# Finer steps of a state-space precomputation in the first MLP, and q times old states for four heads in a row

## The chip, the cores and the metric

The kernel runs on one core of a Trainium2 chip. A core has TensorE (matmuls; PE in the profile, its weight loads PEld), VectorE (DVE), ScalarE (ACT), GpSimd (POOL) and SyncE (SP, which issues most DMAs here). The metric is the device time of one execution in microseconds, the median of the runs.

## The reference

One step of a two-layer decoder: 256 prompt tokens of one sequence and 8 sequences with 4 new tokens each, so 288 columns in all, with 2048 features.

```python
def trunk(x, c, pos, s_gla, s_ret, s5_re, s5_im, ...):
    sc = jax.nn.silu(c)
    for l in range(2):
        mod = jnp.einsum('bd,sde->sbe', sc, w_ada[l]) + b_ada[l][:, None, :]   # shift, scale, gate
        h = modulate(rmsnorm(x, norm_pre[l, 0]), sh0, scl0)
        if l == 0:   # 4 GLA heads and 4 RetNet heads, dk 128, dv 256
            y, ng, nr = gla_retnet_mixer(h, pos, s_gla, s_ret, ...)
        else:        # diagonal complex state space: 128 groups x 64 states
            y, nre, nim = s5_mixer(h, s5_re, s5_im, lam_re, lam_im, log_dt, b, c, d, w_glu_a, w_glu_b)
        x = x + gt0[:, None, :] * rmsnorm(y, norm_post[l, 0])
        h = modulate(rmsnorm(x, norm_pre[l, 1]), sh1, scl1)
        m = jnp.square(jax.nn.relu(h @ w_mlp_up[l])) @ w_mlp_down[l]           # 2048 -> 8192 -> 2048
        x = x + gt1[:, None, :] * rmsnorm(m, norm_post[l, 1])
```

In the mixer of layer 0 each head has a state S (128 x 256) for each sequence. The 4 new tokens of a sequence give `o = att @ v + q_in @ S` and `S = decay * S + k_out^T v`. In layer 1 the discretised coefficients (exp, sin and cos of lambda times dt, their powers and their products with b and c) depend on weights alone; they are computed in the kernel all the same.

## The kernel before

Activations are kept with features on partitions: tiles of 128 x 2 x 288. A weight product is made from three fp32r matmuls (lines 242 to 244: high part by high part, low activation by high weight, high activation by low weight). For that each weight load of 1 MB (512 x 512) is split by ScalarE into `wh` (line 220) and by VectorE, sometimes GpSimd, into `wl` (line 222). **A weight slot** is one such load: 48 matmuls of 128 x 128 by 288 columns, 16 of each line.

The stages in order: condition vectors (`ada_stream`, matmuls of line 254), input projection, attention and output projection of layer 0 (64 slots), the first MLP, the state-space layer, the second MLP.

In these stages the order of TensorE's and SP's instructions is the order of the program text (`manual_schedule`); that of VectorE, ScalarE and GpSimd comes from a planner, which takes what is ready by its own estimates. Each engine then works off its queue in order. Nearly all temporary tiles of 128 x 576 come from one pool, `c2`, of 53 buffers; a new tile waits until the one that had its buffer is done with.

*The first MLP* (`Mlp.run`) has, after a head of 4 slots, 124 slots, here numbered from 0: groups u = 1 to 15 of four "up" slots (n = 0 to 3) and four "down" slots (n = 0 to 3), and four last down slots. After the up slots of a group `hidden` makes relu, its square, and its parts hi and lo (lines 579, 580, 228, 230). In the down slots products are added to accumulators (lines 649 for the first group, 651 after). At fixed places of a slot one step is taken of a generator, `drain(side, 1)`: a step runs up to the next `yield`.

*The side generator* is `s5_pre`, in this order: four steps of small VectorE instructions (128 x 64) that depend on each other; 32 steps (4 groups, 4 powers m, real and imaginary) in each of which GpSimd makes a product `fb` and an array `fz` (lines 1436 to 1442), with TensorE's transposes of `fz` (line 1378), ScalarE's copy `ft`, four DMAs from SP's queue and, for every second, TensorE's lag matmuls (line 1396) with a DMA from GpSimd's queue (line 1406), one or two steps later; then 8 steps of `lc` (lines 1464 to 1467: for each of four powers four products, a sum and a DMA on GpSimd); and 8 steps of tables `tc`, `ts` (lines 1475 to 1490: six doublings of six operations each on GpSimd, two copies and two DMAs).

*Old states* (`samples`, once for GLA and once for RetNet): for each of 4 groups `gb` of two sequences and each of 4 heads, TensorE multiplies q by the old state (line 953, two matmuls of fp32, each recorded as two passes, into the 32 columns of the array that belong to the head) and makes k^T v in PSUM (line 957); VectorE decays the state and adds it (line 961 or 965), GpSimd issues the store (line 966). The masks `km` of a group are two VectorE operations (line 923). The generator `attention` that contains it is advanced by `fill_in`, four times a slot; a step that yields 1.3 uses up 1.3 calls. Steps that are left when the output projection needs the result (ahead of slots 48 and 56 of the 64, numbered from 0) are all taken at once.

Of the kernel before, what the change touches and what calls it, by code (L numbers as in the profile page):

```python
# [13 lines left out]
OP = mybir.AluOpType  # L14
# [9 lines left out]
DK, DV, H = 128, 256, 4  # L24
# [132 lines left out]
def build(tc, nc, d):  # L157
# [27 lines left out]
    def bank(shape=(128, 512)):  # L185
        return bp.tile(list(shape), F32, name=nm("b"), tag="b")
# [311 lines left out]
    class Mlp:  # L498
# [53 lines left out]
        def run(self, r, fill, last=False, side=None, after=None, prep=(None, None)):  # L552
            l = self.l
            sub = Sub(l, 1)
            hid, acc, hv = {}, {}, {}
            slots = []
            for u in range(1, 17):
                slots += [("up", u, n) for n in range(4) if u < 16] + [("dn", u - 1, n) for n in range(4)]
            due = [0.0]

            def fill_in(rate):
                due[0] += rate
                while due[0] > 0:
                    due[0] -= next(fill, None) or 1

            def w_load(i):
                if i < len(slots):
                    k, u, n = slots[i]
                    self.raw[i] = load(d["g_up"][l, u, n] if k == "up" else d["g_dn"][l, n, u])

            def w_split(i):
                if i < len(slots):
                    hv[i] = split_w(self.raw.pop(i))

            def hidden(u, ps):
                hid[u] = []
                for pr in range(2):
                    t = c2("relu")
                    A.activation(t, ps[pr][:, :, :NT], AF.Relu)  # L579
                    V.tensor_mul(t, t, t)  # L580
                    hid[u].append(split_a(t))

            acts, ps = self.head(r, fill)
            with tc.manual_schedule(engines={E_.PE, E_.SP}):
                w_load(0)
                w_load(1)
                w_split(0)
                hidden(0, ps)
                for i, (k, u, n) in enumerate(slots):
                    w_load(i + 2)  # L590
                    w_split(i + 1)
                    if k == "up":
                        for pr in range(2):
                            if n == 0:
                                ps[pr] = pair()
                            gran_mm(ps[pr], hv[i], pr, acts[4 * n:4 * n + 4], n == 0, n == 3)
                            fill_in(0.28 if side else 0.3)
                        if n == 3:
                            hidden(u, ps)
                        if side and n:  # L600
                            drain(side, 1)
                    else:
                        if n == 0:
                            ops = chunks(hid.pop(u))
                        g = kgran_(hv[i], ops, acc, n, u == 0, sub.add if u == 15 else None)
                        for _ in range(2):
                            drain(g, 2)
                            fill_in(0.28 if side else 0.3)
                        if side and n == 1:
                            drain(side, 1)  # L610
                    del hv[i]
                drain(fill)
            if side:
                drain(side)
            return sub.finish(last, fill=after, prep=prep)
# [252 lines left out]
    def samples(kind, qs, ks, kos, dec):  # L868
# [38 lines left out]
                V.tensor_mul(t, q, m)  # L907
            qm.append(t)
        yield
        steps = [(gb, hp) for gb in range(4) for hp in range(2)]  # L910

        def state(n):
            gb, hp = steps[n]
            st = [at("st", shape=(128, 2, DV)) for _ in range(2)]
            for c in range(2):
                nc.sync.dma_start(st[c], src[gb][:, 2 * hp + c])
            return st

        def kmask(gb):
            km = []  # L920
# [19 lines left out]
            A.copy(w_[64:128], w_[0:64].bitcast(F32))  # L940
            vst.append(w_)
        km = kmask(0)
        nxt = state(0)
        yield 2
        os_ = bank((128, DV))
        for n, (gb, hp) in enumerate(steps):
            st = nxt
            if n < 7:
                nxt = state(n + 1)
            for c in range(2):  # L950
                h = 2 * hp + c
                for bb in range(2):
                    mm(os_[32 * h:32 * h + 32, :], qm[hp][:, c, 2 * gb + bb, :], st[c][:, bb, :],
                       start=gb == 0 and bb == 0, stop=False, tile_position=(0, 32 * h))
                ps = bank((128, 2, DV))
                for bb in range(2):
                    mm(ps[:, bb, :], km[bb][:, 128 * h:128 * h + 128], vst[hp][:, 256 * c:256 * c + 256],
                       start=True, stop=True)
                if kind == 0:
                    for bb in range(2):  # L960
                        V.scalar_tensor_tensor(st[c][:, bb, :], st[c][:, bb, :],
                                               dec[:, h, 2 * gb + bb:2 * gb + bb + 1], ps[:, bb, :],
                                               op0=OP.mult, op1=OP.add)
                else:
                    V.scalar_tensor_tensor(st[c], st[c], GAM4[h], ps, op0=OP.mult, op1=OP.add)
                G.dma_start(dst[gb][:, h], st[c])
                if c == 0:
                    yield 1.3
            if hp == 1 and gb < 3:
                km = kmask(gb + 1)  # L970
            yield 1.3
        for h in range(4):
            mm(os_[32 * h:32 * h + 32, :], ats[:, 32 * h:32 * h + 32],
               vst[h // 2].bitcast(F32)[0:64, 256 * (h % 2):256 * (h % 2) + 256], start=False, stop=True,
# [265 lines left out]
    def s5_pre():  # L1240
# [213 lines left out]
        for p in range(8):  # L1454
            ct = c2("ct", shape=(128, 8, 2, 32))
            nc.sync.dma_start(ct, d["cz"][p])
            for t_ in range(4):

                def lb(n):
                    return lam[t_][n][:, 8 * p:8 * p + 8][:, :, None].to_broadcast([128, 8, 32])  # L1460

                o, m = c2("lc", shape=(128, 8, 2, 32)), c2("cm", shape=(128, 8, 2, 32))
                for ri in range(2):
                    G.tensor_mul(o[:, :, ri], ct[:, :, ri], lb(0))
                    G.tensor_mul(m[:, :, ri], ct[:, :, 1 - ri], lb(1 if ri else 2))
                G.tensor_add(o, o, m)
                G.dma_start(s5c[p, t_], o.rearrange("p q r i -> p (q r i)"))
            yield

        for g in range(8):  # L1470
            sl = slice(8 * g, 8 * g + 8)
# [5 lines left out]
            for k in range(6):  # L1477
# [6 lines left out]
                for o, (i0, i1), op in ((tc_, (tc_, tsn), OP.subtract), (tsn, (tsn, tc_), OP.add)):  # L1484
                    G.tensor_mul(m1[:, :, lo], i0[:, :, lo], eb(0))
                    G.tensor_mul(m2[:, :, lo], i1[:, :, lo], eb(1))
                    G.tensor_tensor(o[:, :, hi_], m1[:, :, lo], m2[:, :, lo], op=op)
            for ri, t in enumerate((tc_, tsn)):
                G.tensor_copy(s5end[:, ri, sl], t[:, :, 63])
                G.dma_start(s5tab[2 * g:2 * g + 2, :, ri].rearrange("c p n -> p c n"),  # L1490
# [313 lines left out]
```

## Time and profile before

| | us |
|---|---|
| median of 3 runs | 2963.15 (2962.37 to 2964.34) |
| the profiled execution | 2974.36 |
| its span, first to last instruction | 2972.6 |
| TensorE busy in the span | 2769.6 (93%), mean clock 0.962 |
| VectorE busy | 1686.1 (57%) |
| ScalarE busy | 1102.1 (37%) |
| GpSimd busy | 777.2 (26%) |

The profile is of one execution, some 11 us longer than the median. A line of a timeline gives start and duration in us, engine, source line, operation, output and inputs, shapes and count, and in brackets the idle time before it and who ended it. Matmuls are pipelined: a record of 0.29 us is followed by the next after 0.13. "Clock" is the share of full speed that TensorE was granted in the stretch.

### The profile page before, as it was taken

What the parts mean: (1) busy time and instruction counts of PE and PEld (TensorE: products, weight loads), DVE (VectorE), ACT (ScalarE), POOL (GpSimd) and SP (SyncE); (2) the same over time, 40 slices, a digit from 0 to 9 for tenths busy, and PEclk for the clock granted to TensorE, in tenths of its full rate; (3) what the DMA queues carried; (4) which work ended last, traced back from release to release, by engine and by line L of the source; (5) the groups of instructions that cost most, each with busy time, mean ns of one, the idle gap of its engine ahead of it and who ended that gap; (6) DMA issues with size and microseconds to landing.
All of it is one profiled execution on the core that took longest, in us unless ns stands there. A gap on an engine that the chain in (4) does not pass through costs nothing. (4 is left out here: it accounts for less than half of the span.)

```text
span 2972.6 us, 53134 instructions
## 1 busy us (share of the span) xinstructions
PE 2769.6 (93%) x22262; PEld 2482.0 (83%) x22262; DVE 1686.1 (57%) x2231; ACT 1102.1 (37%) x1447; POOL 777.2 (26%) x1032
## 2 busy tenths in 40 slices
PE   6999999988999999997787879999799999999997
PEld 3878777687899999997787657888599999999997
DVE  2355654546855455466555656766745555555546
ACT  3344424334433333332223344433443333433332
POOL 1333232351223233179994311111200000000002
PEclk8999999998999999999888889999899999999998
DMA  9887777655576766754544587896565444444442
GB/s 346 334 317 295 266 253 279 231 202 200 227 247 243 255 242 237 255 200 156 192 145 144 178 274 264 312 326 224 203 242 198 169 168 160 169 167 160 169 168 91
DMA packets 164208, 662.09 MB, mean 223 GB/s; under 512 B 21104, under 2 KB 40944, under 8 KB 104576
## 3 DMA queue, kind: packets, MB, share of 16 engines
q1 hardware_dynamic: 154976, 632.67, 59.3%
q0 software_dynamic: 7840, 23.67, 2.0%
q8 instruction: 174, 2.85, 0.4%
q10 hardware_dynamic: 1152, 2.36, 0.2%
q14 instruction: 66, 0.54, 0.1%
HBM read 621.86 MB, written 36.77 MB: 222 GB/s over the span
## 5 line engine op out<-in xcount | busy, mean ns | idle before, releaser
L242 PE MATMUL mm<-hi,wh 128*128 128x288 f32 x5632 | 1700.5, 302 | 93.5 <-ACT relu L579 35.3
L244 PE MATMUL mm<-hi,wl 128*128 128x288 f32 x5632 | 1674.9, 297 | 4.9 <-DVE wl L222 4.5
L243 PE MATMUL mm<-lo,wh 128*128 128x288 f32 x5632 | 1675.2, 297 | 2.5 <-DVE lo L230 2.1
L242 PEld LDWEIGHTS mm<-hi,wh 128*128 128x128 f32 x5632 | 1069.2, 190 | 229.9 <-issue 85.3
L222 DVE TENSOR_TENSOR wl<-raw,wh 128x1024 fp32r<-128x1024 f32 x630 | 821.4, 1312 | 666.0 <-ACT wh L220 646.2
L220 ACT CAST wh<-raw 128x1024 fp32r<-128x1024 f32 x704 | 730.2, 1047 | 1114.3 <-PE mm L243 892.0
L244 PEld LDWEIGHTS mm<-hi,wl 128*128 128x128 f32 x5632 | 1069.9, 190 | 6.6 <-DVE wl L222 6.0
L243 PEld LDWEIGHTS mm<-lo,wh 128*128 128x128 f32 x5632 | 1071.0, 190 | 3.6 <-DVE lo L230 2.3
L651 DVE TENSOR_TENSOR acc<-acc,mm 128x576 f32<-128x576 f32 x304 | 227.8, 750 | 158.4 <-PE mm L244 158.1
L222 POOL TENSOR_TENSOR wl<-raw,wh 128x1024 fp32r<-128x1024 f32 x74 | 188.7, 2552 | 418.2 <-ACT wh L220 390.3
L463 POOL TENSOR_TENSOR acc<-acc,modG 128x512 f32<-128x512 f32 x32 | 42.5, 1328 | 906.1 <-ACT sq L382 902.2
L254 PE MATMUL b<-raw,cpad 128*32 128x512 f32 x1152 | 162.6, 638 | 25.2 <-DMA raw<-g_ada 25.2
L230 DVE TENSOR_TENSOR lo<-relu,hi 128x576 fp32r<-128x576 f32 x64 | 71.2, 1112 | 59.7 <-ACT hi L228 26.4
L580 DVE TENSOR_TENSOR relu<-relu 128x576 f32<-128x576 f32 x64 | 60.4, 944 | 78.5 <-ACT relu L579 78.2
L228 ACT CAST hi<-relu 128x576 fp32r<-128x576 f32 x64 | 43.2, 675 | 115.2 <-DVE relu L580 70.1
L1406 POOL DMA_DIRECT2D s5k<-lag x16 | 12.6, 790 | 264.4 <-ACT lag L1405 209.2
L579 ACT ACTIVATE relu<-mm 128x576 f32<-128x576 f32 x64 | 41.5, 648 | 107.4 <-PE mm L244 79.5
L254 PEld LDWEIGHTS b<-raw,cpad 128*32 128x32 f32 x1152 | 23.2, 110 | 59.7 <-issue 33.6
L1436 POOL TENSOR_TENSOR fb<-bt,t 128x256 f32<-128x256 f32 x32 | 26.3, 821 | 162.3 <-DVE t L1367 81.9
L1201 DVE TENSOR_TENSOR acc<-acc,mm 128x576 f32<-128x576 f32 x40 | 30.0, 751 | 59.6 <-PE mm L244 59.6
L1442 POOL TENSOR_TENSOR fz<-fb 64x256 f32<-64x256 f32 x64 | 59.9, 935 | 3.4
L254 PE MATMUL b<-adaw,cpad 128*32 128x512 f32 x384 | 56.5, 636 | 0.6 <-DMA adaw<-g_ada 0.6
(323 smaller groups left out, 1801.9 us busy)
## 6 DMA issues: line engine op xcount, KB each, us to landing
raw<-g_ada SPq DMA_DIRECT2D x144, 1024.0 KB, 5.2
raw<-g_up SPq DMA_DIRECT2D x128, 1024.0 KB, 4.9
raw<-g_dn SPq DMA_DIRECT2D x128, 1024.0 KB, 4.9
raw<-g_in SPq DMA_DIRECT2D x48, 1024.0 KB, 7.0
adaw<-g_ada SPq DMA_DIRECT2D x192, 256.0 KB, 6.2
raw<-g_glu SPq DMA_DIRECT2D x64, 512.0 KB, 6.6
raw<-g_out SPq DMA_DIRECT2D x16, 1024.0 KB, 6.0
s5b<-ft SPq DMA_DIRECT2D x128, 64.0 KB, 4.6
```

Source lines behind the costliest of these rows:

```text
L220: A.copy(wh, r)
L222: (lo[hf] or V).tensor_sub(wl, r, wh.bitcast(F32))
L228: A.copy(hi, t)
L230: V.tensor_sub(lo, t, hi.bitcast(F32))
L242: mm(o, wh[:, k4 % 2, cs], hi, start=first and k4 == 0, stop=False)
L243: mm(o, wh[:, k4 % 2, cs], lo, start=False, stop=False)
L244: mm(o, wl[:, k4 % 2, cs], hi, start=False, stop=last and k4 == nk - 1)
L254: mm(ps[32 * k4:32 * k4 + 32, :], cpad[:, 4 * kg + k4, 18 - 9 * slot:50 - 9 * slot], raw[k4] if isinstance(raw, list) else raw[:, k4, :], ...
L463: G.tensor_mul(t[:, :, :NP], t[:, :, :NP], self.g[:, 2 * p:2 * p + 2, 0:1].to_broadcast([128, 2, NP]))
L580: V.tensor_mul(t, t, t)
L651: V.tensor_add(acc[pi], acc[pi], ps[:, :, :NT])
L1442: G.tensor_add(z[ks, :, k], m[ks, 0], m[ks, 1])
```

## The change

Two things are changed. In the first MLP the side generator is stepped after all four up slots of a group (before: three) and after three of its down slots (before: one), and its last two parts yield more often: after each power of `lc` (32 steps, before 8) and two more times within each table, after the second and the fourth doubling (24 steps, before 8). In `samples` the loads, products and yields are put in another order: first q times old state for all four heads of a group and for its two sequences, the heads taken in turn; then a step; then, head by head and each with a step, k^T v, the update, the store and the load of the next group's state. A group has five steps of 1.3 (before four); a head's state for the next group is loaded right after its update (before: two heads at a time, one pair ahead).

```diff
-                        if side and n:
+                        if side:
                             drain(side, 1)
...
-                        if side and n == 1:
+                        if side and n < 3:
                             drain(side, 1)
...
-        steps = [(gb, hp) for gb in range(4) for hp in range(2)]
-
-        def state(n):
-            gb, hp = steps[n]
-            st = [at("st", shape=(128, 2, DV)) for _ in range(2)]
-            for c in range(2):
-                nc.sync.dma_start(st[c], src[gb][:, 2 * hp + c])
-            return st
+
+        def state(gb, h):
+            t = at("st", shape=(128, 2, DV))
+            nc.sync.dma_start(t, src[gb][:, h])
+            return t
...
-        nxt = state(0)
+        st = [state(0, h) for h in range(4)]
         yield 2
         os_ = bank((128, DV))
-        for n, (gb, hp) in enumerate(steps):
-            st = nxt
-            if n < 7:
-                nxt = state(n + 1)
-            for c in range(2):
-                h = 2 * hp + c
-                for bb in range(2):
-                    mm(os_[32 * h:32 * h + 32, :], qm[hp][:, c, 2 * gb + bb, :], st[c][:, bb, :],
+        for gb in range(4):
+            for bb in range(2):
+                for h in range(4):
+                    mm(os_[32 * h:32 * h + 32, :], qm[h // 2][:, h % 2, 2 * gb + bb, :], st[h][:, bb, :],
                        start=gb == 0 and bb == 0, stop=False, tile_position=(0, 32 * h))
+            yield 1.3
+            for h in range(4):
+                hp, c = divmod(h, 2)
                 ps = bank((128, 2, DV))
...
-                G.dma_start(dst[gb][:, h], st[c])
-                if c == 0:
-                    yield 1.3
-            if hp == 1 and gb < 3:
-                km = kmask(gb + 1)
-            yield 1.3
+                G.dma_start(dst[gb][:, h], st[h])
+                if gb < 3:
+                    st[h] = state(gb + 1, h)
+                    if h == 3:
+                        km = kmask(gb + 1)
+                yield 1.3
...
                 G.dma_start(s5c[p, t_], o.rearrange("p q r i -> p (q r i)"))
-            yield
+                yield
...
                     G.tensor_tensor(o[:, :, hi_], m1[:, :, lo], m2[:, :, lo], op=op)
+                if k in (1, 3):
+                    yield
```

## Rows read from the trace of the kernel before

**Rows 1.** The page: POOL's busy tenths in 40 slices of 74.3 us.

```profile
POOL 1333232351223233179994311111200000000002
```

**Rows 2.** Stretches: start:end, length, busy us of each engine (count), clock, DMA share, GB/s.

```profile
360.00:430.00 70.00, 70.00 (x463) 55.37 (x462) 33.84 (x68) 20.27 (x27) 24.76 (x23) 1.00 0.76 265
737.00:789.00 52.00, 52.00 (x390) 47.98 (x389) 49.01 (x202) 22.04 (x27) 0.00 (x0) 1.00 0.64 241
1279.00:1340.00 61.00, 59.07 (x482) 58.35 (x469) 46.15 (x37) 20.39 (x23) 57.41 (x63) 1.00 0.57 209
1340.00:1456.00 116.00, 80.87 (x539) 78.68 (x540) 73.76 (x45) 28.71 (x31) 111.97 (x130) 0.87 0.46 172
1456.00:1600.00 144.00, 112.67 (x772) 111.44 (x771) 78.63 (x58) 38.04 (x40) 134.60 (x338) 0.86 0.42 149
2400.00:2800.00 400.00, 400.00 (x3015) 400.00 (x3014) 216.25 (x219) 151.20 (x158) 0.00 (x0) 1.00 0.46 166
```

**Rows 3.** Stretches, instructions of line 243 alone (every third weight matmul).

```profile
1279.00:1681.00 402.00, 237.14 (x781) 153.86 (x781) 0.91 0.46 168
2400.00:2800.00 400.00, 296.50 (x1005) 188.74 (x1005) 1.00 0.46 166
```

**Rows 4.** Waits (us, times, longest) in 1279:1600; then TensorE's timeline.

```profile
PE mm L242 <- ACT relu L579: 34.9, 5, 17.9
PE mm L242 <- DVE acc L651: 31.9, 10, 10.8
...
ACT relu L579 <- POOL lc L1466: 26.5, 2, 21.2
...
1424.94 0.61 PE L242 MATMUL mm<-hi,wh 128*128 128x288 f32 x1 [17.89 <-ACT relu L579]
```

**Rows 5.** Lines 1467 and 1490: ns min/median/max, first and last start us.

```profile
L1467 POOL DMA_DIRECT2D s5c<-lc x32: 581/581/593, 1289.1 to 1456.9; - x32
...
L1490 POOL DMA_DIRECT2D s5tab<-ts x8: 725/740/751, 1492.5 to 1596.7; - x8
```

**Rows 6.** Line 222 in 737:789; then timelines of DVE, ACT, POOL and PE.

```profile
L222 DVE TENSOR_TENSOR wl<-raw,wh 128x1024 fp32r<-128x1024 f32 x14 | 17.1, 1220 | 0.0
...
737.42 0.20 DVE L1248 TENSOR_SCALAR t<-s5v 128x64 f32<-128x64 f32 x1 [0.56 <-DMA s5v<-s5v]
...
768.14 0.63 ACT L649 COPY acc<-mm 128x576 f32<-128x576 f32 x1
...
789.17 0.66 POOL L1436 TENSOR_TENSOR fb<-bt,t 128x256 f32<-128x256 f32 x1 [81.88 <-DVE t L1367]
...
794.20 1.55 POOL L1442 TENSOR_TENSOR fz<-fb 64x256 f32<-64x256 f32 x2
...
806.30 1.04 PE L1378 MATMUL b<-idn,fz 128*128 128x128 f32 x8
```

**Rows 7.** TensorE's timeline: old states in RetNet; a condition block.

```profile
572.81 0.50 PE L957 MATMUL b<-vst,km 128*128 128x256 f32 x2
...
574.84 1.05 PE L953 MATMUL b<-st,qm 128*32 128x256 f32 x4
575.82 0.50 PE L957 MATMUL b<-vst,km 128*128 128x256 f32 x2
...
701.43 1.06 PE L254 MATMUL b<-raw,cpad 128*32 128x512 f32 x8
```

**Rows 8.** DVE's timeline; landing of tile st; lines 792 and 823 (start range).

```profile
576.36 0.69 DVE L965 SCALAR_TENSOR_TENSOR st<-st,b 128x512 f32<-128x512 f32 x1 [0.79 <-PE b L957]
...
578.38 0.88 DVE L923 TENSOR_SCALAR km<-kst,cst 128x512 fp32r<-128x512 f32 x2
...
DMA to landing us min/median/max: 2.2/6.9/10.7
...
L792 DVE TENSOR_TENSOR rr<-rr,rt x4: 757/758/2941, 436.9 to 451.5; 128x576 f32<-128x576 f32 x4
...
L823 PE MATMUL b<-rr,rr x8: 377/377/379, 456.7 to 519.2; 128*128 128x256 f32 x8
```

More of the change, by code (lines that the diff above doesn't have):

```diff
@@ L960, in samples @@
                     for bb in range(2):
-                        V.scalar_tensor_tensor(st[c][:, bb, :], st[c][:, bb, :],
+                        V.scalar_tensor_tensor(st[h][:, bb, :], st[h][:, bb, :],
                                                dec[:, h, 2 * gb + bb:2 * gb + bb + 1], ps[:, bb, :],
@@ L964, in samples @@
                 else:
-                    V.scalar_tensor_tensor(st[c], st[c], GAM4[h], ps, op0=OP.mult, op1=OP.add)
-                G.dma_start(dst[gb][:, h], st[c])
-                if c == 0:
-                    yield 1.3
-            if hp == 1 and gb < 3:
-                km = kmask(gb + 1)
-            yield 1.3
+                    V.scalar_tensor_tensor(st[h], st[h], GAM4[h], ps, op0=OP.mult, op1=OP.add)
+                G.dma_start(dst[gb][:, h], st[h])
[4 more added lines that the diff above has]
+                yield 1.3
         for h in range(4):
```

## The prediction

> **What bounds the kernel now.** Four views were read, from coarse to fine.
>
> First POOL's strip on the page [rows 1]: GpSimd is a third busy or less nearly everywhere, but in the slices from about 1260 to 1600 us it is at nine tenths. Second, the stretches [rows 2]. In 1340:1456 and 1456:1600 POOL is busy 112.0 of 116 and 134.6 of 144 us, while TensorE is busy only 80.9 and 112.7, at a granted clock of 0.87 and 0.86. In 2400:2800, the same MLP code of the second layer without side work, TensorE is busy 400 of 400 at clock 1.00. In 360:430, the old states of GLA, TensorE is busy 70 of 70: there TensorE itself is the bound. Third, the matmuls of line 243, a third of all weight matmuls [rows 3]: 1005 in 400 us is 0.398 us for each, so a weight slot (16 of them) needs 6.37 us undisturbed. The 49 slots between 1279 and 1681 would need 49 x 6.37 = 312 us and took 402. **90 us are lost there.** Fourth, the waits of that stretch [rows 4]: TensorE waits 34.9 us for ScalarE's relu and 31.9 us for VectorE's accumulation; behind these, ScalarE waits for POOL's `lc` (26.5 us of relu alone), and the longest pause, 17.89 us up to 1424.94, ends with such a relu. The reason is in the code: relu, hi and lo take buffers of the pool `c2`, which POOL's tables still hold. The 67 us idle and the half-speed matmuls after each pause make up the 90.
>
> So POOL is late, not overloaded: its work for the state-space layer is issued in eight-fold portions at the end, after slot 75, and then runs without a break until slot 110.
>
> **Part 1: finer steps of the state-space precomputation.** Counting the yields and the places where they are drained: before, four places in eight slots and 54 steps, the POOL-heavy ones after slots 75 to 106. After, seven places in eight slots and 94 steps: coefficients (`lc`, 32 steps) after slots 43 to 78, tables (24 thirds) after slots 80 to 106. No instruction is added.
>
> *POOL's load.* The 32 `lc` steps took 1289.1 to 1456.9 [rows 5], 31 intervals of 5.4 us; the eight tables from there to 1596.7, 17.5 us each. Per eight slots (51 us) POOL now gets 7 x 5.4 = 38 us, then 7/3 x 17.5 = 41 us: 75% and 80%. VectorE, beside which these durations were taken, was busy 59% in 1340:1600 and is busy 54% in the undisturbed MLP [rows 2], so they should not grow. POOL then stays within one or two steps of TensorE, where before it fell some 50 us behind (the last `lc` is drained after slot 90; the long pause stands ahead of slot 92 [rows 4], so slot 90 ended at 1424.9 - 17.9 - 6.4 = 1400.6, and that `lc` was issued at 1456.9). I take 88 of the 90 us back; bounds 50 and 90.
>
> *The start of the chain.* This is what the finer steps cost. The chain is about 200 small VectorE instructions, then two POOL products, then transposes of these on TensorE, whose order is written by hand: TensorE cannot pass them. Before, the drains lie after slots 1, 2, 3, 5 (VectorE), 9, 10 (POOL) and 11 (transposes). After, they lie after 0, 1, 2, 3, 4, 5 and 6. VectorE's chain begins at 737.42 and lets POOL start at 789.17; the first two products end at 795.75; TensorE's transposes come at 806.30, without a wait [rows 6]. VectorE is busy 49.0 of 52 us in between [rows 2], 17.1 of them for splits of weights [rows 6], so some 30 us are the chain itself and it cannot be compressed much. Begun one slot (7 us) earlier, it gives the products at about 789. But the transposes now stand behind slot 6, whose second half is evicted at 768.14 [rows 6]. That is a new wait of 21 us, less some 3 us because VectorE gets no new MLP work while TensorE stands, plus 2 us of matmuls at half clock behind it: **20 us lost**, bounds 0 (VectorE takes the chain first) and 26. Everything on TensorE is queued behind it: slots 7 and on, and with them the splits on ScalarE and VectorE.
>
> *The transposes and lags after that* come every second slot instead of every fourth. POOL's pair of products takes 6.6 us [rows 6], two slots 12.7; and the products of a step are issued well ahead of its transposes, so I set 4 us for all further small waits; bounds 0 and 20 (half a microsecond for each of 30). The saves to HBM of each transpose (SP's queue) and the table writes (POOL's) keep their number and move earlier; SP passes its weight loads in the same order, only closer together, in a stretch where the DMA engines are busy 64% [rows 2].
>
> Part 1: 88 - 20 - 4 = **64 us gained**, bounds 20 and 90.
>
> **Part 2: q times old states, four heads in a row.** In the GLA and RetNet samples a head's block costs TensorE as follows [rows 7]. From state product to state product (572.81 to 575.82) there are 3.01 us with 12 weight matmuls in between, 12 x 0.1325 = 1.59, so the block is 1.42 us; the q part of it from 574.84 to 575.82 is 0.98 us and about 0.1 to enter. Its four records start one behind the other, because consecutive ones use the same 32 columns of the array. The condition block at 701.43 has four column groups in a row, two passes of 512 columns each, and its eight records take 1.06 us together. The new row of a group of two sequences has 4 heads x 2 x 2 passes of 256 columns: the same columns in the same groups. I price it at 1.2 us; bounds 1.06 and 3.9 (no overlap at all). For the state product alone, without the change of tile shape, 0.34 us a head is left. Before: 4 x 1.42 = 5.7 us a group; after 1.2 + 4 x 0.34 = 2.6; **3.1 us saved, eight times: 25 us**. In GLA's stretch TensorE is the bound, so 12 us are path.
>
> In RetNet a part is lost again. The steps cost 1.3 units each and there are now 20 instead of 16. For GLA the extra 5 units are taken up, since `ret_heads` waited for projections anyway; RetNet's are not, so nine heads and two rows, instead of seven heads, are left for the point ahead of slot 55 where all remaining steps run in one go. There VectorE decides: 0.69 us a head and 0.88 us for the two masks of a group [rows 8], 9 x 0.73 + 2 x 0.9 + 1 = 9.4 us, where TensorE has only 9 x 0.34 + 2 x 1.2 = 5.5. So 4 us of RetNet's 12.5 are lost. The Trainium skill has this as a rule, in TensorEngine Tiling (Array Packing), PSUM Bottleneck: tiling speeds up TensorE, but not the emptying of PSUM. By that rule alone the other heads would go at VectorE's pace too (rival 3); the trace has VectorE busy 33.8 of 70 us in GLA's stretch [rows 2], so there it leaves room.
>
> RetNet's rotations now start 1.5 slots closer to their first use (last product 451.5, first matmul 456.7 [rows 8]); 2 us, bounds 0 and 8. The next group's state is loaded one step ahead of its use instead of two; a load lands in 6.9 us (10.7 at most) [rows 8], a step is 1.6 to 3 us, and SP runs ahead of TensorE by an amount that no row here gives: taken at nothing, at worst 2 us for each of six rows.
>
> Part 2: 25 - 4 - 2 = **19 us gained**, bounds 0 and 27.
>
> **Sum.** 64 + 19 = 83 us. The profiled execution took 2974.36 us (span 2972.6), 11 us above the median of 2963.15; the difference is taken from both: 2891 in a profile, 2880 in the median.
>
> **Rivals.**
> 1. *The wait at the first transposes is hidden*, because VectorE's order puts the chain ahead of the MLP's splits. For it: VectorE's queue is planned, not written by hand. Against it: before, splits stood amid the chain and it took 52 us. 2880 - 22 = 2858.
> 2. *Buffers still bind*: tables come in unequal thirds (the last third has the two largest sizes), and a relu still waits now and then for one. For it: 80% load leaves little slack. Against: in 1279:1340, with POOL already busy 57.4 of 61 us, TensorE still worked 59.1 [rows 2], so the buffers bear a good lag. Half of the loss stays, 2880 + 40 = 2920.
> 3. *Part 2 gives little.* If every head went at VectorE's pace, 0.73 us and 0.22 for its share of the masks, and the row's 0.3 on top, it would take 1.25 instead of 1.42: 32 x 0.17 = 5 us, so 2880 + 14 = 2894; if the rows did not overlap at all, 2899.
> 4. *Slower*: TensorE's hand-written order waits at nearly every pair of transposes. Place: POOL's queue, in which the write of a lag result (it waits for TensorE and ScalarE) can stand ahead of both products of the next transposes. It decides once the pair behind that write (6.6 us) must fit between two drains one slot (6.4 us, 7.4 with a condition block) apart, not three. Then some 4 us and 4 us at half clock for each of 15 pairs: 2880 + 120 = 3000. Against: at the start of the chain the second pair of products follows the first at once, ahead of any write: at 806.30 TensorE's transposes waited for nothing [rows 6].
> 5. *No gain from part 1*, POOL as late as before and the first wait on top: 2963 + 20 - 19 = 2964.
>
> **Chances.** Forecast 0.52; rival 1 0.13; rival 2 0.13; rival 3 0.12; rival 4 0.05; rival 5 0.05. The range 2848 to 2925 holds the first four. A difference of 0.2% (6 us) is about what can be told from no change. Faster 0.90, same 0.03, slower 0.07.
>
> **What would show it.** POOL's strip spread evenly over 800 to 1520 at six to eight tenths, with no stretch at nine; the 49 slots from slot 75 on in about 315 us; one gap of TensorE of some 18 us ahead of the first transposes of `fz`, in the first eight slots; the q records in rows of 16 lasting 1.0 to 1.3 us. Wrong would be: waits of relu for `lc` or `tc` of over 20 us in total, gaps ahead of many transposes, or q rows of 3 us and more.

## The result and the profile after

| | before | after |
|---|---|---|
| median of four runs on one chip | 2963.11 us | 2912.52 us (2908.73 to 2916.80) |
| ratio, 95% interval | | 0.9829, 0.9812 to 0.9846 |
| profiled execution (span) | 2974.36 us (2972.6) | 2908.73 us (2907.0) |

The change makes the kernel 50.6 us faster, where 83 were predicted (2880 us, range 2848 to 2925). Between the two profiled executions it is 65.6 us; of the other 15, 11.2 are what the execution before lay above its median and 3.8 what the one after lay below.

GpSimd's strip after (40 slices of 72.7 us; [rows 1] before), from the page:

```profile
POOL 1333232342244446679940310103100000000003
```

The work now begins some 200 us earlier and rises evenly to seven tenths, but two slices, 1308 to 1453, are still at nine. Stretches after, columns as in [rows 2]: the old states of GLA, the start of the first MLP, its slots 7 to 75 and its slots 75 to 124; then the last of these for line 243 alone, as in [rows 3]:

```profile
356.00:416.00 60.00, 59.42 (x471) 52.92 (x465) 33.58 (x58) 20.90 (x26) 24.26 (x21) 1.00 0.86 301
707.00:773.00 66.00, 52.00 (x378) 46.66 (x375) 59.12 (x218) 25.49 (x31) 6.84 (x11) 0.93 0.59 221
773.00:1297.00 524.00, 513.33 (x4727) 474.30 (x4726) 279.35 (x265) 178.32 (x216) 283.46 (x334) 0.99 0.72 253
1297.00:1614.00 317.00, 314.82 (x2354) 314.01 (x2353) 192.15 (x186) 118.64 (x126) 193.53 (x374) 0.99 0.50 178
...
1297.00:1614.00 317.00, 231.71 (x782) 147.56 (x781) 0.99 0.50 178
```

The 49 slots that took 402 us [rows 3] now take 317, and TensorE is busy 314.8 of them at clock 0.99. All that it waits for in them, against the 34.9 and 31.9 us of [rows 4]:

```profile
PE mm L244 <- DVE wl L222: 1.1, 1, 1.1
PE mm L242 <- ACT wh L220: 1.1, 1, 1.1
```

The price stands at the first transposes (TensorE's timeline), which had waited for nothing before [rows 6]:

```profile
759.54 0.29 PE L244 MATMUL mm<-hi,wl 128*128 128x288 f32 x1
770.32 1.11 PE L1374 MATMUL b<-idn,fz 128*128 128x128 f32 x4 [10.49 <-POOL fz L1438]
772.54 1.11 PE L1374 MATMUL b<-idn,fz 128*128 128x128 f32 x4 [1.11 <-POOL fz L1438]
773.30 0.59 PE L242 MATMUL mm<-hi,wh 128*128 128x288 f32 x1
```

The granted clock is 0.50 from 764 to 777 (TensorE had stood idle since 759.8): the matmul at 773.30 takes 0.59 us, four transposes 1.11.

In the attention stage, the q row of RetNet's first group, undisturbed, and then the burst ahead of slot 55 (against [rows 7]):

```profile
533.39 1.07 PE L946 MATMUL b<-st,qm 128*32 128x256 f32 x16
...
558.48 0.62 PE L946 MATMUL b<-st,qm 128*32 128x256 f32 x2
561.14 0.62 PE L946 MATMUL b<-st,qm 128*32 128x256 f32 x2 [2.04 <-DMA st<-s_ret]
562.57 1.06 PE L946 MATMUL b<-st,qm 128*32 128x256 f32 x2 [0.81 <-DMA st<-s_ret]
567.66 1.92 PE L946 MATMUL b<-st,qm 128*32 128x256 f32 x10 [4.03 <-DMA st<-s_ret]
```

A row of 16 records takes 1.07 us (1.2 was the estimate), where four records took 1.05 before. In the burst the next group's row stands for its states three times, 6.9 us, at half clock behind that. TensorE's largest waits in 400:590:

```profile
PE b L946 <- DMA st<-s_ret: 6.9, 3, 4.0
PE b L979 <- DVE ons L852: 4.4, 1, 4.4
PE b L979 <- DVE ons L862: 3.3, 1, 3.3
PE b L1008 <- DVE att L826: 2.2, 1, 2.2
```

The second line is GLA's normalised output. VectorE's timeline shows why it is late: RetNet's rotations now stand amid the small steps of that norm, and the first of them waits for a table.

```profile
426.67 0.75 DVE L788 TENSOR_TENSOR rt<-acc,cst 64x576 f32<-64x576 f32 x1 [3.45 <-DMA cst<-cst]
427.44 0.75 DVE L789 TENSOR_TENSOR rt<-acc,cst 64x576 f32<-64x576 f32 x1
428.22 0.16 DVE L836 RECIPROCAL sr<-ss 128x1 f32<-128x1 f32 x1
...
430.37 0.48 DVE L852 SCALAR_TENSOR_TENSOR ons<-b,sr,gns 128x256 f32<-128x256 f32 x1
```

**Where the time went, by stretches.** TensorE's order is written by hand, so the kernels can be laid beside each other slot by slot: every slot has 48 weight loads of lines 242 to 244, and it starts with the first of them. Column A runs from the start of slot 34 of the attention stage to slot 0 of the first MLP, B from slot 4 to slot 8 of it (the first transposes), C from slot 8 to 75, D from 75 to 123. What lies ahead of A, slots 0 to 3 and what lies behind D differ by under 5 us each. In us, one execution of each kernel:

| kernel (label) | A | B | C | D | ratio to before (95%) |
|---|---|---|---|---|---|
| before | 358.2 | 27.9 | 504.8 | 395.4 | 1 |
| after | 351.0 | 45.2 | 514.4 | 310.6 | 0.9829 |
| after, again (f1_full_again) | 345.3 | 47.6 | 512.6 | 323.3 | 0.9833 (0.9811 to 0.9856) |
| part 1 alone (e1_part1) | 355.6 | 44.8 | 515.0 | 323.3 | 0.9874 (0.9851 to 0.9897) |
| part 2 alone (e2_part2) | 347.1 | 27.9 | 504.1 | 389.2 | 0.9974 (0.9963 to 0.9986) |
| part 2 alone, 1.04 units (g2_part2_104) | 332.7 | 27.9 | 501.0 | 387.7 | 0.9930 (0.9916 to 0.9944) |
| full, 1.04 units (e4_yield104) | 335.6 | 45.8 | 513.3 | 311.4 | 0.9803 (0.9776 to 0.9830) |
| full, states earlier (f4_early_states) | 348.4 | 45.5 | 514.9 | 307.7 | 0.9789 (0.9760 to 0.9819) |
| full, later start (e3_late) | 343.8 | 27.9 | 521.4 | 335.0 | 0.9845 (0.9824 to 0.9866) |
| full, one product buffer (g3_full_serial) | 347.3 | 45.2 | 519.0 | 309.2 | 0.9818 (0.9804 to 0.9831) |
| full, later start, one buffer (f2_late_serial) | 348.4 | 27.9 | 514.9 | 308.8 | 0.9747 (0.9728 to 0.9766) |
| the same with 1.04 units (g1_late_serial_104) | 333.8 | 27.9 | 516.1 | 310.3 | 0.9728 (0.9713 to 0.9743) |
| before, one buffer (f3_before_serial) | 357.7 | 27.9 | 502.9 | 377.5 | 0.9956 (0.9941 to 0.9971) |
| full, drains only, steps whole (h1_places_only) | 348.3 | 46.4 | 600.4 | 306.4 | 1.0095 (1.0067 to 1.0122) |

After against before: A -7.2, B +17.3, C +9.6, D -84.8; the rest -0.5; together -65.6.

### The profile page after: what moved, and what is told of

Its sections match the earlier page's. It is cut to its first block, busy times and chain, and to the rows that moved or that the text cites. A ratio compares the mean times of both kernels' runs of the same rounds, so it can differ in the third digit from the quotient of the medians.

```text
span 2907.0 us, 53144 instructions
## 1 busy us (share of the span) xinstructions
PE 2741.7 (94%) x22262; PEld 2471.2 (85%) x22262; DVE 1658.7 (57%) x2231; ACT 1101.4 (38%) x1447; POOL 804.2 (28%) x1032
## 4 chain that ended last, share of the span: by engine, by line
PE 84%; DVE 7%; DMA 4%; ACT 2%; issue 2%; POOL 1%; SPq 0%; DVEq 0%; ACTq 0%; POOLq 0%
PE mm L242 25%; PE mm L244 24%; PE mm L243 24%; PE b L254 6%; DVE wl L222 1%; PE b L1559 1%; DVE acc L482 1%; DMA x<-xT 1%; DMA cst<-cst 1%; PE b L1620 1%; ACT h L1549 1%; DMA raw<-g_up 1%; DVE x L483 1%; ACT wh L220 1%; PE b L1625 1%
## 5 line engine op out<-in xcount | busy, mean ns | idle before, releaser
L580 DVE TENSOR_TENSOR relu<-relu 128x576 f32<-128x576 f32 x64 | 52.0, 813 | 70.9 <-ACT relu L579 70.9
L230 DVE TENSOR_TENSOR lo<-relu,hi 128x576 fp32r<-128x576 f32 x64 | 52.2, 815 | 29.9 <-ACT hi L228 28.7
L1460 POOL TENSOR_TENSOR lc<-ct,t 128x256 f32<-128x256 f32 x48 | 38.8, 808 | 70.4 <-DMA ct<-cz 69.2
L1438 POOL TENSOR_TENSOR fz<-fb 64x256 f32<-64x256 f32 x64 | 53.2, 832 | 3.6
```

The source lines that it names most:

```text
L230: V.tensor_sub(lo, t, hi.bitcast(F32))
L1438: G.tensor_add(z[ks, :, k], m[ks, 0], m[ks, 1])
```

## The experiments

**The two parts by themselves.** Part 1 alone is the kernel before with these edits:

```
-                        if side and n:
+                        if side:
...
-                        if side and n == 1:
+                        if side and n < 3:
...
-            yield
+                yield
...
+                if k in (1, 3):
+                    yield
```

> Part 1 alone: the finer yields of the precomputation and the seven drain places, with the samples of the kernel before. Reading the traces of before and after slot by slot, part 1 is worth about 57 us of profile (85 us won in slots 75 to 124, 13.6 lost at the first transposes, 11.4 lost in slots 7 to 75); of the 50.6 us by which the medians differ that leaves 42 to 50, so 2913 to 2921 us. The prediction's own terms say 2963 - 64 = 2899. Rival: part 2 costs more than it brings; then this kernel is faster than the full change, under 2908. In the trace: first MLP slots 75 to 124 in 315 to 318 us, and a pause of about 10 us ahead of the first transposes of fz.

Measured: 2931.93 us against 2966.3, ratio 0.9874: 34 us of median. B and C cost 17 and 10 us as in the full change, D took 323.3. That is less than the 42 to 50 expected (the interval goes from 31 to 44); the pause ahead of the first transposes was there (10.96 us).

Part 2 alone is the change without those lines.

> Part 2 alone: q times old states for four heads in a row, 1.3 units for each of 20 steps, the first MLP stepped as before. By the two traces its net gain at the start of the first MLP is about 7 us: 2956 us, 0.2 per cent. The prediction's own terms say 2963 - 19 = 2944. Rival: it gives nothing or less, 2963 or over. In the trace: the waits of TensorE for st come from the load from s_ret again (some 7 us) and the q rows ahead of slot 55 run at half clock.

Measured: 2957.84 us, ratio 0.9974, or 8 us less; A took 347.1, 11 us less than before. The waits came at the places expected: 4.7 us for the states of RetNet (7 were expected), and 4.8 for `ons`. Together the parts give 43 of the full change's 50 us, a difference that the intervals cover: both terms of the prediction were too large, 64 and 19, and no interaction of the two is shown.

**Part 2: the plan, not the products.** In the full change:

```
-            yield 1.3
+            yield 1.04
...
-                yield 1.3
+                yield 1.04
```

> The full change, with 1.04 units in place of 1.3 for each of the 20 steps of a samples generator, so that a group of two sequences takes 5.2 units of the plan, as it did before. Theory: the extra 1.3 units a group pushed the end of GLA's samples against RetNet's rotations (4.4 us wait of TensorE for ons, 2.2 us for att, with half clock behind them) and left nine heads for the burst ahead of slot 55; with them gone, 6 to 12 us less than the full change: 2900 to 2906 us. Rival: the waits for the state loads from s_ret (7 us) set the loss of RetNet whatever the units are, and GLA's tail is a matter of VectorE's order; then within 3 us of the full change.

Measured: 0.9803, some 8 us less than the full change, though the intervals overlap; A took 335.6, 10 to 15 us less. TensorE's three largest waits in 400:590:

```profile
PE b L979 <- DVE ons L862: 3.3, 1, 3.3
PE b L1023 <- DVE on L862: 1.9, 1, 1.9
PE b L946 <- DMA st<-s_ret: 1.4, 1, 1.4
```

The 4.4 us for `ons` and 2.2 for `att` are gone, and with them all but 1.4 of the 6.9 us for the states. The rival, that the waits for states stay, fell. But the burst ahead of slot 55 is still there, with two rows and one head less; what changed is when its states are loaded. SyncE's timeline, in the full change and then here:

```profile
545.53 0.37 SPq L913 DMA_DIRECT2D st<-s_ret  x1
554.52 0.33 SPq L331 DMA_DIRECT2D raw<-g_ada  x1
554.90 0.90 SPq L913 DMA_DIRECT2D st<-s_ret  x2
...
541.89 2.43 SPq L913 DMA_DIRECT2D st<-s_ret  x4
548.97 2.01 SPq L913 DMA_DIRECT2D st<-s_ret  x4
```

In the full change the queue stands for 8.6 us ahead of the weight load at 554.52, which waits for TensorE's line 254, and three of the four states for the row at 558.48 come behind it. With 1.04 units the states of both rows are on their way by 551, ahead of the burst. From the last weight load ahead of the burst to the next one it is 23.4 us in the full change, 14.7 here and 15.7 before.

The same units with part 2 alone give its price without any of part 1:

> Part 2 alone with 1.04 units for each step, so that only the order of the products differs from the kernel before and the plan of the attention stage does not. By the prediction's price of the rows (3.1 us a group, eight times) 25 us, by the trace of e4_yield104 ahead of the first MLP 22: 2938 to 2943 by 2963, ratio 0.991 to 0.993. Rival: e4_yield104 was a lucky execution, and part 2 is worth no more than the 0.3 per cent of e2_part2: ratio 0.996 to 0.998.

Measured: ratio 0.9930, 21 us; in A 25.5 us. From slot 34 to 41 (GLA's four groups) it is 59.9 us against 71.7, so 11.8 for four groups, and the other four make up the rest. That is close to the 3.1 us a group of the prediction. Here the intervals are apart from those of e2_part2, so the units count.

Loading the states earlier, instead:

```
+            nxt = [state(gb + 1, h) for h in range(4)] if gb < 3 else None
             yield 1.3
...
-                if gb < 3:
-                    st[h] = state(gb + 1, h)
-                    if h == 3:
-                        km = kmask(gb + 1)
+                if gb < 3 and h == 3:
+                    km = kmask(gb + 1)
+                    st = nxt
```

> The full change, with the four states of the next group loaded right behind the q row of the group before, into four more buffers, instead of one behind each head. Theory: TensorE's three waits for st ahead of slot 55 (2.0, 0.8 and 4.0 us) come from loads that are issued too late; they go, and the half clock behind them (562 to 576) with them: 8 to 11 us less than the full change, 2902 to 2905 by the kernel before at 2963. Rival: SP stands behind weight loads that wait for a buffer, and all loads of a burst are issued at its start anyway; or VectorE's rotations set the pace of the burst: then within 3 us of the full change.

The median (2907.01, ratio 0.9789) is about where the theory put it, but the trace says that the edit did not do what it was meant to do: A took 348.4 us, and the waits stand:

```profile
PE b L946 <- DMA st<-s_ret: 5.6, 4, 2.4
PE b L979 <- DVE ons L852: 4.7, 1, 4.7
```

The row that takes 6.9 us of waits in the full change now waits for nothing, but the one behind it waits 5.6 us in four pieces. Its four loads go out together, right behind two weight loads that went out only at 554.3 and 554.8:

```profile
555.19 2.25 SPq L913 DMA_DIRECT2D st<-s_ret  x4
```

That is the first of the two rivals named: SyncE stands behind weight loads, and the edit only moved the late loads to the other side of that stand. In A this execution lies between the full change's two (351.0 and 345.3); D, which the edit does not touch, is 307.7 against 310.6 and 323.3. The interval overlaps that of the full change, too. A median alone would have credited the edit.

**The first transposes.** In the full change the first 16 slots drain where they did before:

```
-                        if side:
+                        if side and (n if u <= 2 else True):
...
-                        if side and n < 3:
+                        if side and (n == 1 if u <= 1 else n < 3):
```

> The full change, but in the first 12 slots of the first MLP the drains stand where they stood before (after slots 1, 2, 3, 5 and then 9, 10, 11), and at seven of eight places only after that. Theory: the pause ahead of the first transposes of fz (10.5 and 1.1 us, and 13.7 us of half clock) comes only from where these transposes stand in TensorE's hand-written order; here it is gone, and the end of the tables moves by some six slots, which no one waits for: 13 us less than the full change, 2899 us. Rival: VectorE's chain is what is late and holds up the splits of weights wherever the transposes stand; then the pause only changes its name, and the time is 2908 to 2915.

Measured: 0.9845, no gain at all. B is back at 27.9, so the pause came from the places of the drains (it did not change its name); but C took 521.4, 7 to 9 us more, and D 335.0, 12 to 24 us more than in the full change. One instruction shows what happened in D, on VectorE:

```profile
1370.65 10.02 DVE L222 TENSOR_TENSOR wl<-raw,wh 128x1024 fp32r<-128x1024 f32 x1 [1.78 <-ACT wh L220]
1380.59 0.74 DVE L651 TENSOR_TENSOR acc<-acc,mm 128x576 f32<-128x576 f32 x1
```

The split takes 1.22 us elsewhere [rows 6]. The full change itself, run again, has the same:

> The full change once more, unchanged, beside the three kernels that follow, so that they can be compared with it on one chip. Expected: 0.983 of the kernel before, in whose trace of the tables of the first MLP no VectorE instruction with both operands in SBUF lasts over 2.5 us.

Measured: 0.9833 as expected, but against the expectation two splits of 8.86 and 7.36 us in the tables, where the first execution had none over 2 us. VectorE, then GpSimd, then TensorE, around the first:

```profile
1418.82 8.86 DVE L222 TENSOR_TENSOR wl<-raw,wh 128x1024 fp32r<-128x1024 f32 x1 [1.83 <-ACT wh L220]
1427.61 0.74 DVE L651 TENSOR_TENSOR acc<-acc,mm 128x576 f32<-128x576 f32 x1
```

```profile
1418.66 0.29 POOL L1481 TENSOR_TENSOR m<-ts,s5E 128x64 f32<-128x64 f32 x1
1418.92 0.29 POOL L1482 TENSOR_TENSOR m<-tc,s5E 128x64 f32<-128x64 f32 x1
...
1425.99 0.61 POOL L1482 TENSOR_TENSOR m<-tc,s5E 128x256 f32<-128x256 f32 x1
1426.55 1.18 POOL L1487 COPY s5end<-tc 128x8 f32<-128x8 f32 x1
1427.68 0.75 POOL L1488 DMA_DIRECT2D s5tab<-tc  x1
```

```profile
1428.40 0.61 PE L242 MATMUL mm<-hi,wh 128*128 128x288 f32 x1 [5.83 <-DVE acc L651]
```

From 1418.92 on, 18 products and sums of GpSimd follow one another without a gap (each starts before the record of the one ahead of it has ended: two tables are woven into one another, so none waits for its predecessor). The split ends 1.1 us after the row does, beside a copy that takes 1.18 us (0.18 for the next); the accumulation is queued behind the split, and TensorE stands 5.83 us. In the five executions of woven kernels with these places and portions, D goes with such holds: 310.6, 311.4 (e4_yield104) and 307.7 us (f4_early_states) where no split of the tables lasts over 3.5 us, 323.3 here and 323.3 in e1_part1, which has two of 9.05 and 5.93.

**Unweaving the tables.** If every product writes the same buffer, GpSimd can't start the next table before the last one is summed:

```
+            if not p:
+                cm1 = c2("cm", shape=(128, 8, 2, 32))
...
-                o, m = c2("lc", ...), c2("cm", ...)
+                o, m = c2("lc", ...), cm1
...
-            m_ = c2("m1", shape=(128, 2, 8, 32))
-            m1, m2 = m_[:, 0], m_[:, 1]
+            m1, m2 = (... the two halves of cm1 ...)
```

The first of these kernels has the later start of e3_late as well:

> The later start of the chain (label e3_late), and one buffer for the products of all coefficients and tables (cm, m1) in place of one each, so that GpSimd can't weave several tables into one another. Theory: in e3_late the 13 us won at the first transposes were given back in the tables, where VectorE's splits were held for 10.0 and 7.1 us while GpSimd ran woven products back to back (and for 6.6 and 6.5 us in the coefficients). With each table's products depending on the one before there are gaps, no VectorE instruction of L222, L230 and L580 lasts over 4 us, and slots 84 to 104 take 128 us in place of 144: 2893 to 2902 us in all (by the kernel before at 2963). Rival: a load of GpSimd of three quarters, not the weaving, is what makes TensorE wait; then slots 84 to 104 keep their 140 us and the time stays at 2912 to 2918.

Measured: 2891.45 us, ratio 0.9747; D fell from e3_late's 335.0 to 308.8, where 48 undisturbed slots of 6.37 us would take 306. Slots 84 to 104 took the 128 us expected. GpSimd in a table of this kernel, then VectorE:

```profile
1402.80 0.40 POOL L1483 TENSOR_TENSOR cm<-ts,s5E 128x128 f32<-128x128 f32 x1
1403.28 1.33 POOL L1484 TENSOR_TENSOR tc<-cm 128x128 f32<-128x128 f32 x1
1404.69 0.40 POOL L1482 TENSOR_TENSOR cm<-ts,s5E 128x128 f32<-128x128 f32 x1
...
1403.01 1.28 DVE L222 TENSOR_TENSOR wl<-raw,wh 128x1024 fp32r<-128x1024 f32 x1 [1.83 <-ACT wh L220]
```

The sum starts 0.08 us after the products it needs; VectorE's split is done in 1.28 us, and it is GpSimd's sum beside it that takes 1.33 instead of 0.45. In the tables no split lasts over 2.22 us. In the coefficients, which still have rows of independent products, the expectation failed: one of 6.62 us at 1113. The rival, that GpSimd's load is what counts, fell: in its tables (1343:1524) GpSimd is busy 166.1 of 181 us, in those of f1_full_again (1315:1477) 152.0 of 162.

> The full change with one product buffer for coefficients and tables, and nothing else. It divides f2_late_serial's gain of 26 us over the full change between its two edits. If the holds of VectorE are what the full change loses in the tables (10 us of the difference of two of its executions), this one gains 6 to 14 us on it (ratio 0.978 to 0.981), slots 75 to 124 take 308 to 312 us, and the later start is worth the remaining 12 to 18. Rival: only the later start counts; then ratio 0.983, as the full change.

Measured: 0.9818 (2907.92 to 2913.14 in five runs), D 309.2, but C 519.0, 5 us more. The one buffer alone is worth 3 to 4 us, which the intervals don't tell from nothing, where 6 to 14 were expected; the other 21 us of f2_late_serial's 25 are the later start, more than the 12 to 18 expected, because B costs 17 to 20 and C is 4 us shorter. With the later start and the woven tables (e3_late) there is no gain: in these runs each needs the other.

> The kernel before, with nothing changed but that one buffer (cm1) holds the products of all coefficients and tables: no finer steps, no earlier drains. It tells apart two readings of the 90 us lost in slots 75 to 124. Reading of the prediction (GpSimd starts too late, and its tables hold the buffers): GpSimd has as much to do and starts no earlier, so 2963, within 8 us. The other reading (GpSimd weaves four and five tables into one another, so that VectorE finds no gap and none of the tables gets finished and gives its buffers back): the long pauses shrink, slots 75 to 124 take some 370 us in place of 402, and the time is 2925 to 2940.

Measured: 2954.72 us, ratio 0.9956; 13 us, between the two readings (under 8, or 23 to 38). D went from 395.4 to 377.5, but TensorE's long waits remain:

```profile
PE mm L242 <- DVE acc L651: 26.9, 7, 10.3
PE mm L242 <- ACT relu L579: 26.8, 2, 13.8
```

Weaving was the smaller part of the 90 us (10 to 18 by D, beside the three kernels of the table that step the first MLP as before); the prediction's reading keeps the larger. What the one buffer does to the number of buffers held was not separated from what it does to VectorE.

**Finer steps or earlier drains?** The full change with the two added yields taken out again, so that a step is four coefficients or a table:

```
-                yield
+            yield
...
-                if k in (1, 3):
-                    yield
```

> The full change with its drains at seven of eight places, but with the steps of the kernel before: a step gives out four coefficients (some 22 us of GpSimd) or a whole table (17.5 us). It tells the finer steps from the earlier drains. Reading of the prediction: GpSimd gets 22 us of work at each slot of 6.4 to 7.4 us, falls behind and holds the buffers, so the long pauses ahead of relu come back, only some 25 slots earlier, and with less of the tail to catch up: slots 43 to 75 take 50 to 90 us longer than in the full change, and the time is 2950 to 2990. Rival: it is enough that the work is given out early, whatever the portions; then within 10 us of the full change.

Measured: 2995.08 us, ratio 1.0095: slower than before, and 78 us slower than the full change by the ratios. GpSimd's strip, then timelines of SyncE, ScalarE and TensorE:

```profile
POOL 1332232350344469993000211111300000000002
...
1161.18 0.33 SPq L1452 DMA_DIRECT2D ct<-cz  x1
1161.60 0.38 SPq L212 DMA_DIRECT2D raw<-g_dn  x1
...
1167.69 1.99 ACT L220 CAST wh<-raw 128x1024 fp32r<-128x1024 f32 x2 [16.97 <-DMA raw<-g_dn]
1179.10 0.65 ACT L579 ACTIVATE relu<-mm 128x576 f32<-128x576 f32 x1 [9.42 <-POOL lc L1462]
...
1179.80 0.61 PE L242 MATMUL mm<-hi,wh 128*128 128x288 f32 x1 [38.24 <-ACT relu L579]
```

The block of nines has only moved some 215 us ahead (from 1337 to 1560 to 1121 to 1345), and a pause ahead of `relu` is there again, 38 us where 17.9 was the longest before. Only 9.4 of these are `relu`'s wait for `lc`; ahead of it ScalarE had waited 20.0 and 17.0 us for weight loads. Those stand in SyncE's queue behind the loads of `ct`, the input of the coefficients, which need a buffer of `c2` as well: the queue stood at `ct` for 91 us in 1060:1340. In the kernel before it stood there for 79 us in 1279:1620, in the full change in 1060:1340 not at all. So the buffers that GpSimd holds late reach TensorE by two ways, `relu` and the weight loads; which share of the 90 us came by which was not separated.

The earlier drains by themselves gain nothing: part 1 needs the small portions. That the small portions would do without the added places was not run (94 steps do not fit into the some 60 places of the kernel before).

**Together.** Later start, one buffer and 1.04 units:

> The later start of the chain, one product buffer for coefficients and tables (label f2_late_serial), and 1.04 units for each step of the samples (label e4_yield104). If what the runs so far showed is three separate losses, f2_late_serial's 0.975 of the kernel before and the 12 us that e4_yield104 had at the start of the first MLP add up: 0.970 to 0.972 of the kernel before, 2875 to 2880 us by 2963, which is what was predicted for the change itself. Rival: RetNet's shorter burst is taken up again further on; then 0.974 to 0.976.

Measured: 2884.01 us (2881.22 to 2888.04), ratio 0.9728: 82 us off the kernel before and the fastest of all, by 30 us on the full change. It missed the expected 0.970 to 0.972 by a little: A gave 14.6 us on f2_late_serial, but the rest of the execution took 5 back. The intervals of the two overlap.

## Why the prediction was right and wrong

- **Direction, range and place held.** The gain comes from the slots behind 75 of the first MLP, and GpSimd's large portions were what cost the time (h1_places_only), as far as the runs tell portions and places apart. Beside the buffers of `relu`, which the prediction names, SyncE's `ct` loads waited for these buffers too, with the weight loads behind them. The 49 slots take 317 us; 315 were said.
- **The 88 us taken back were 85 in one execution, 72 in the next.** The step that failed is "VectorE, beside which these durations were taken, ... so they should not grow". They grew: the products and sums of the coefficients from 156.8 to 164.6 us in all, those of the tables from 125.2 to 148.8. So the strip still has two slices at nine, against the words of the forecast. And the step asks how busy VectorE is, not who holds whom: in some executions a split is held by a row of products, and with that goes the 13 us between the two D. In the kernel before it varies too: 387.7 and 389.2 us in the two kernels that step the first MLP as it does, 395.4 in the profile from which the 90 was read. By these two, some 7 of the 90 us were that one execution's, and of the 11 us by which it lay above the median most lie here; to take these off both kernels' times alike, and the gain in full, was the mistake.
- **The new wait of 20 us** was right in size: B costs 16.9 to 19.7, in all kernels with the early drains (44.8 to 47.6 against 27.9). It was sized as a wait of 21 less 3 plus 2 at half clock; it is a wait of 12 and the rest mostly in matmuls at half clock. That the chain "cannot be compressed much" held only in part: it took 47.5 us (718.34 to 765.81) where it took 51.8, and began 11 us behind the start of slot 0 where it had begun 20 behind; one slot, 7 us, was counted. So rival 1, that VectorE takes the chain first, came true for some 6 us of the wait. (Its 2858 takes off 22 us, where the term is 20.)
- **"4 us for all further small waits"** was 8 to 10 (C), within its bounds. Half of it is one wait, 4.8 us for `acc` up to 1252.6, behind a split of 6.56. Another 4.8 us are waits for `wl`.
- **Part 2's price of the products was right, its place in the plan was not.** 25 us were counted, and g2_part2_104 shows 25.5 in A. In GLA's groups VectorE did not bind: 11.8 of 12 us were gained there. So the rule of the Trainium skill weighed in the prediction (TensorEngine Tiling (Array Packing), PSUM Bottleneck) did not come to bear in them. But the full change keeps only 7 to 13. Two terms failed: GLA's five extra units, "taken up" by waits for projections, push the end of GLA's samples against RetNet's rotations, 4.4 and 2.2 us of waits and half clock behind them; and RetNet's nine heads in one burst cost more than VectorE's 4 us, because the state loads, "taken at nothing", cost 6.9 us there. They are late because SyncE comes to them late, from behind a weight load that goes out at 554.52, just ahead of the burst. A lead of a whole row did not help (f4_early_states); the plan that let them out at 541.9 to 551 did (e4_yield104).
- **Rival 2,** that a `relu` still waits for buffers, did not come: in 1297:1614 TensorE waits 2.2 us in all, none of it for `relu` (in f1_full_again 2.5 for `relu`). **Rival 4, slower,** did not come from the transposes; the slower outcome that was near is the one of h1_places_only, and it was not among the rivals.

The sum, in profiles: 19 became 7, 20 became 17, 4 became 10, 88 became 85: 83 became 65. With the executions' means (10, 18, 9, and 390 less 317 for D) it is some 56, close to the 50.6 of the medians.

## What to carry to other kernels

Side work that shares buffers with the main chain should be handed out in small portions: the same work drained early in large portions was slower than before, in small ones 78 us faster than that. Look then at every queue that asks for these buffers, the one that issues the loads too. When a step is split, keep the sum of its planned units (20 times 1.04, not 20 times 1.3), or the plan runs late and gives the gain back at the next forced finish. And lay kernels beside each other by the start of each slot: it found the holds, and it kept a median 11 us lower from being put down to an edit that had gained nothing in the stretch it touched.

## What the runs showed of the hardware

A VectorE instruction with both operands in SBUF stood for 5 to 10 us beside GpSimd products that followed one another without a gap (`wl` up to 10.02 us, the square of `relu` 7.12, both in e3_late; `lo` 5.22 in f1_full_again), while `acc` (one operand in PSUM) took 0.74 to 0.76 us in all executions of the same stretch. Of this the Trainium skill (SBUF — State Buffer, Who interferes with whom) says that such an instruction contends with a GpSimd instruction that reads SBUF. Its rules for kernel authors (the Trainium skill, SBUF — State Buffer, Summary) add that the second one to issue is blocked until the first has finished. Which instructions are hit agrees; but here VectorE was kept out for a row of 18 instructions (8.86 us), not for one, until GpSimd came to the copy behind the row (in the coefficients, as with this `lo`, to a DMA issue). With the same order of GpSimd's instructions one execution of the full change had such holds in the tables and another none; what decides it stays open.
